# Block boundaries with rstd and the scaled product in PSUM, the residual add on VectorE, and sums of squares as float32 products

## The chip, the cores and the metric

One core of a Trainium2 chip runs the whole program. The metric is the time of one execution on the device, in microseconds (us). TensorE multiplies matrices from SBUF into PSUM (8 banks of 128 x 512 float32), VectorE and ScalarE work on SBUF and PSUM, GpSimd on SBUF; DMA queues bring the weights.

## What is computed

Two blocks follow each other on 512 tokens of width 1024, in float32. The first has two layers of this form, with four gains each:

```python
h = rms_norm(x, g[0])
m = parallel_conv_mla(h, ...) if i % 2 == 0 else conformer_conv(h, ...)
x = x + rms_norm(m, g[1])
h = rms_norm(x, g[2])
x = x + rms_norm(squared_relu_mlp(h, w1[i], w2[i]), g[3])
```

`rms_norm(x, g)` is `x * rsqrt(mean(x * x) + 1e-6) * g`, the mean over the 1024 channels. The second block is one layer with a forgetting attention, a pooled branch and a gated MLP; it takes the first block's `x`.

## The kernel before

Activations lie channel by channel: 8 tiles of 128 channels x 512 tokens. A product in float32 precision is three TensorE matmuls, because every operand is kept as a high part and a low part of a narrower format: high x high, high x low, low x high (`mm3`, L357 to L359). The split of an activation is a ScalarE copy that makes the high part (L397, or L400 with a scale) and a VectorE subtraction that makes the low part (L398, L401). Weights come by DMA as `raw`, and are split the same way (L284 on ScalarE, L286 on VectorE, in the conformer's stage on GpSimd) into nine buffers `W`.

`boundary` (L929) stands between two sublayers and runs four times: behind the attention (`mla`), behind the first MLP, behind the conformer, behind the second MLP. It gets the residual `x`, the sublayer's output `m` with its last three tiles still to be multiplied (`last`), and `acc`, the squares of the first five tiles, summed over the tiles. It works on the left 256 tokens (`LA`) and the right 256 (`LB`) in turn:

- TensorE multiplies the last three tiles for the left half, and starts on the first for the right half. The evacuations add their squares to `acc`; the third tile's squares stay apart (`sq[0]`).
- `parts` splits `acc` (L397, L398), `sums` (L960) multiplies the high part, the low part and `sq[0]` by a matrix of ones (L962, L963, L964): the sum over the channels stands in every partition.
- `rsqrts` (L405) makes `r = rsqrt(sum / 1024 + eps)`: ScalarE's table function (L450 through `fn`), then one Newton step in three VectorE instructions (L420, L422, L424).
- `update` (L967) forms `m * g * r` on VectorE (L970) and adds it to `x` (L973): on GpSimd for all left tiles, and for the right tiles 3, 5, 6, 7; on VectorE for the right tiles 0, 1, 2, 4 (`XB`). `update2` splits the new `x`, scaled by the next norm's gain, into `h` (L400, L401) and asks for one more block of weights.
- TensorE, done with the last three tiles, starts the next sublayer's first four weight tiles (`first`, in four PSUM banks): `kouter` runs over k = 0 to 7 for the left half, and behind k = 2 calls `hook`, then over k = 0 to 7 for the right half. `hook` holds the right half's sum, the left updates of tiles 4 to 7, the right rsqrt, the eight right updates, and the squares of the new `x`: `acc2`, left half added on GpSimd (L470), right half on VectorE.
- `acc2` gives the next sublayer its norm (`rs`) later, by `rstd_acc` and `colsum` (L459, L460), behind one more weight tile's 24 matmuls. Until then the first products wait unscaled in PSUM.

Instructions are put in each engine's order at compile time: among those whose inputs are ready by the compiler's own clock, the one written first goes first; each engine then runs its list strictly in order. A PSUM tile (`PS`) takes one of eight banks, and a bank is free when the tile's last reader is done. `S` are nine SBUF buffers of 128 x 544 for passing values.

Of the kernel before, what the change touches and what calls it, by code (L numbers as in the profile page):

```python
# [16 lines left out]
OP = mybir.AluOpType  # L17
# [4 lines left out]
T = 512  # L22
D = 1024
# [31 lines left out]
XA = ()  # L55
XB = (0, 1, 2, 4)
HK = 2
LA = slice(0, 256)
# [4 lines left out]
LB = slice(256, 512)  # L63
# [180 lines left out]

class Weights:
# [58 lines left out]
class Program:  # L304
# [100 lines left out]
    def rsqrts(self, jobs):  # L405
# [12 lines left out]
        stt = nc.vector.scalar_tensor_tensor  # L418
# [4 lines left out]
        for (s, n, out), q in zip(jobs, qs):  # L423
            stt(out=out, in0=q, scalar=1.5, in1=out, op0=OP.add, op1=OP.mult)  # L424

    def rsqrt(self, s, n, out):
        self.rsqrts([(s, n, out)])
        return out
# [500 lines left out]
    def boundary(self, x, m, acc, last, gi, nxt, first, extra=None):  # L929
# [8 lines left out]
        r, acc2 = self.S()[:, :T], self.S()[:, :T]  # L938
# [18 lines left out]
        def parts(cols):  # L957
            return self.split(self.P(), acc[:, cols], cols=256), sq[0]

        def sums(p, s):  # L960
            ps = self.PS()[:, :256]
            mm(ps, self.ones, p[:, 0, :256], start=True, stop=False)  # L962
            mm(ps, self.ones, p[:, 1, :256], start=False, stop=False)  # L963
            mm(ps, self.onesf, s, start=False, stop=True)  # L964
            return ps

        def update(k, cols):  # L967
            if cols is LA:
                h.append(self.P())
            V.scalar_tensor_tensor(out=m[k][:, cols], in0=m[k][:, cols], scalar=self.v("g", 8 * gi + k),  # L970
                                   in1=r[:, cols], op0=OP.mult, op1=OP.mult)
            eng = V if k in (XA if cols is LA else XB) else G
            ins = eng.tensor_add(out=x[k][:, cols], in0=x[k][:, cols], in1=m[k][:, cols]).ins  # L973
            if eng is G:
                self.last_update = ins
# [17 lines left out]
        s = sums(*parts(LA))  # L993
        tile(0, LB, slice(5, None), pb[0])
        self.rsqrt(s, D, r[:, LA])
# [5 lines left out]
        box = {"p": parts(LB)}  # L1001

        def hook():
            box["s"] = sums(*box["p"])
            updates(range(4, 8), LA)
            self.rsqrt(box["s"], D, r[:, LB])
            updates(range(8), LB)
            for k in range(8):
                self.square_into(acc2[:, LA], x[k][:, LA], k == 0, G)
            for k in range(8):  # L1010
                self.square_into(acc2[:, LB], x[k][:, LB], k == 0)
# [731 lines left out]
```

## Time and profile before

| | us |
|---|---|
| median of three runs (lowest, highest) | 1763.58 (1763.04, 1767.39) |
| the profiled execution | 1762.84 |
| its span, first to last instruction | 1761.1 |
| TensorE busy | 1724.0 (98%) |
| VectorE busy | 1091.2 (62%) |
| ScalarE busy | 801.6 (46%) |
| GpSimd busy | 274.0 (16%) |

Busy time of TensorE is modelled at the ends of its matmuls, so the starts are what to compare. A line number names the instruction's line in the kernel; a helper's line (L398, L401, L470) is shared by all its callers, and the tile names and shapes tell them apart. PE is TensorE, DVE VectorE, ACT ScalarE, POOL GpSimd. In a list in order of time, the bracket gives the engine's idle time before the instruction and what ended it. The four boundaries lie at about 218 to 264, 575 to 623, 785 to 830 and 1143 to 1192 us of the span.

### The profile page before, as it was taken

The numbers are of one execution on the slowest core, as the hardware profiler recorded it, in microseconds if no ns is written. First come the engines' busy times: TensorE is split into PE (matmuls) and PEld (weight loads), VectorE is DVE, ScalarE is ACT, GpSimd is POOL, SyncE is SP. The second block draws the span as 40 slices with busy tenths as digits, with TensorE's granted clock in tenths as the row PEclk, the third lists the DMA queues.
The fourth block names the chain that finished last, engine by engine and source line by source line (L and its number), as shares of the span: only waits on it lengthen the run. The fifth ranks groups of instructions, "written<-read, shape, count | busy, mean of one in ns | idle before, by whom it ended". The sixth has DMA issues, their size and how long they took to land.

```text
span 1761.1 us, 23142 instructions
## 1 busy us (share of the span) xinstructions
PE 1724.0 (98%) x8828; PEld 1460.4 (83%) x8828; DVE 1091.2 (62%) x1772; ACT 801.6 (46%) x1461; POOL 274.0 (16%) x339
## 2 busy tenths in 40 slices
PE   9999999999999999999999999989999999999999
PEld 7778898888888878999888888888787888888887
DVE  7988786344444789968544444488897655344452
ACT  6546655333333446676533333357665443232331
POOL 3513330000000365503000000051223200000000
PEclk9999999999999999999999999999999999999999
DMA  5231313222222133512322222222223222222221
GB/s 198 73 104 55 108 51 130 96 96 96 96 96 96 48 108 107 169 60 85 109 97 96 96 96 96 96 96 74 73 62 101 100 97 98 96 96 96 96 96 60
DMA packets 49887, 167.26 MB, mean 95 GB/s; under 512 B 6848, under 2 KB 7296, under 8 KB 49776
## 3 DMA queue, kind: packets, MB, share of 16 engines
q1 hardware_dynamic: 47776, 160.70, 27.9%
q0 software_dynamic: 1936, 5.07, 0.9%
q8 instruction: 69, 1.13, 0.3%
q14 instruction: 42, 0.34, 0.1%
q10 hardware_dynamic: 64, 0.02, 0.0%
HBM read 158.25 MB, written 4.19 MB: 92 GB/s over the span
## 4 chain that ended last, share of the span: by engine, by line
PE 81%; DVE 11%; issue 3%; ACT 2%; POOL 2%; DMA 1%; SPq 0%; POOLq 0%; ACTq 0%; DVEq 0%
PE ps L357 26%; PE ps L358 26%; PE ps L359 26%; DVE P L970 1%; PE ps L625 1%; DVE W L286 1%; POOL P L973 1%; DVE P L401 1%; DVE S L1479 1%; DVE S L424 1%; DVE P L398 1%; DVE S L422 1%; DMA raw<-in_w 1%; ACT S L450 0%; DVE S L420 0%
## 5 line engine op out<-in xcount | busy, mean ns | idle before, releaser
L357 PE MATMUL ps<-P,W 128*128 128x512 f32 (+1 forms) x2541 | 928.7, 366 | 4.9 <-DVE S L1132 2.8
L358 PE MATMUL ps<-P,W 128*128 128x512 f32 (+1 forms) x2541 | 925.7, 364 | 4.9 <-DVE P L401 4.9
L359 PE MATMUL ps<-P,W 128*128 128x512 f32 (+1 forms) x2541 | 923.9, 364 | 0.0
L284 ACT ACTIVATE W<-raw 128x512 fp32r<-128x512 f32 x578 | 356.6, 628 | 649.9 <-PE ps L359 608.5
L286 DVE TENSOR_TENSOR W<-raw,W 128x512 fp32r<-128x512 f32 x523 | 371.0, 717 | 378.7 <-ACT W L284 376.1
L357 PEld LDWEIGHTS ps<-P,W 128*128 128x128 f32 x2541 | 482.6, 190 | 82.5 <-DVE S L1132 3.2
L358 PEld LDWEIGHTS ps<-P,W 128*128 128x128 f32 x2541 | 482.7, 190 | 79.9 <-DVE P L401 5.7
L359 PEld LDWEIGHTS ps<-P,W 128*128 128x128 f32 x2541 | 482.6, 190 | 75.3 <-DVE W L286 0.2
L973 POOL TENSOR_TENSOR P<-P 128x256 f32<-128x256 f32 x48 | 46.7, 981 | 770.6 <-DVE P L970 769.5
L398 DVE TENSOR_TENSOR P<-S,P 128x512 fp32r<-128x512 f32 (+3 forms) x134 | 93.8, 706 | 50.4 <-ACT P L397 49.8
L397 ACT ACTIVATE P<-S 128x512 fp32r<-128x512 f32 (+3 forms) x134 | 81.5, 614 | 63.8 <-DVE S L1666 25.9
L286 POOL TENSOR_TENSOR W<-raw,W 128x512 fp32r<-128x512 f32 x55 | 72.9, 1348 | 38.1 <-ACT W L284 34.0
L1084 DVE SCALAR_TENSOR_TENSOR ps<-P,vec,ps 128x512 f32<-128x512 f32 x116 | 77.8, 744 | 0.0
L400 ACT ACTIVATE P<-P,vec 128x256 fp32r<-128x256 f32 (+1 forms) x80 | 43.7, 550 | 51.8 <-POOL P L973 31.4
L1031 DVE SCALAR_TENSOR_TENSOR S<-ps,S 128x512 f32<-128x512 f32 x64 | 43.6, 689 | 34.2 <-PE ps L359 34.1
L401 DVE SCALAR_TENSOR_TENSOR P<-P,vec 128x256 fp32r<-128x256 f32 (+1 forms) x80 | 54.3, 692 | 10.9 <-ACT P L400 10.7
L470 POOL TENSOR_TENSOR S<-S 128x256 f32<-128x256 f32 (+1 forms) x45 | 48.7, 1084 | 74.6 <-ACT S L469 72.2
L469 ACT ACTIVATE S<-P 128x256 f32<-128x256 f32 (+1 forms) x105 | 46.4, 472 | 17.4 <-DVE P L1058 11.4
L638 POOL TENSOR_TENSOR P<-S,P 128x512 fp32r<-128x512 f32 (+1 forms) x24 | 34.3, 1427 | 114.4 <-DVE P L637 108.5
L1051 DVE TENSOR_TENSOR P<-ps,P 128x512 f32<-128x512 f32 x42 | 29.0, 691 | 28.7 <-PE ps L359 28.7
L625 PE MATMUL ps<-P 128*128 128x512 f32 (+3 forms) x160 | 41.2, 376 | 2.2 <-DVE S L1445 0.9
L470 DVE TENSOR_TENSOR S<-S 128x256 f32<-128x256 f32 (+1 forms) x60 | 33.1, 551 | 14.4 <-ACT S L469 13.4
(264 smaller groups left out, 1299.8 us busy)
## 6 DMA issues: line engine op xcount, KB each, us to landing
raw<-in_w SPq DMA_DIRECT2D x286, 512.0 KB
P<-in_xT SPq DMA_DIRECT2D x8, 256.0 KB
P<-in_xT POOLq DMA_DIRECT2D x8, 256.0 KB, 5.3
keep<-P SPq DMA_DIRECT2D x8, 256.0 KB
P<-P SPq DMA_DIRECT2D x16, 128.0 KB
P<-keep POOLq DMA_DIRECT2D x8, 256.0 KB, 4.3
out<-P SPq DMA_DIRECT2D x7, 256.0 KB
raw<-in_w SPq DMA_DIRECT2D x2, 256.0 KB
```

What stands on the lines that cost most here:

```text
L284: nc.scalar.activation(out=w[:, 0, :cols], in_=r, func=AF.Copy)
L286: eng.tensor_sub(out=w[:, 1, :cols], in0=r, in1=w[:, 0, :cols].bitcast(F32))
L357: mm(ps, w[0], x[0], start=first, stop=False)
L358: mm(ps, w[0], x[1], start=False, stop=False)
L359: mm(ps, w[1], x[0], start=False, stop=last)
L397: nc.scalar.activation(out=hi, in_=src, func=AF.Copy)
L398: nc.vector.tensor_sub(out=lo, in0=src, in1=hi.bitcast(F32))
L401: nc.vector.scalar_tensor_tensor(out=lo, in0=src, scalar=scale, in1=hi.bitcast(F32), op0=OP.mult, op1=OP.subtract)
L470: (eng or nc.vector).tensor_add(out=acc, in0=acc, in1=t)
L625: mm(o[:m], k, q[:, pl, c0:], start=n == 0 and m == 128, stop=n == len(keys) - 1 and mask is None)
L973: ins = eng.tensor_add(out=x[k][:, cols], in0=x[k][:, cols], in1=m[k][:, cols]).ins
L1084: V.scalar_tensor_tensor(out=dst if dst is not None and t == taps[-1] else acc, in0=u, scalar=w, in1=acc, op0=OP.mult, op1=OP.add)
```

## The change

`r` becomes a PSUM tile; a second PSUM tile, `tm`, takes the product `m * g * r`, and `m` is no longer overwritten. The Newton steps work on an SBUF buffer and only the last writes `r`. The add to `x` is VectorE's for all tiles and both halves, reading `tm`. `sums` multiplies `acc` itself, unsplit, with the float32 ones, so that `parts` is gone; a float32 operand is not two matmuls here but one float32 product. The squares of the left half of the new `x` are added on VectorE too. In `boundary`, GpSimd has no instruction left.

```diff
--- before.py
+++ after.py
@@ -52,8 +52,6 @@
 WARM = 11
 TICK = (6, 3)
 AK = 7
-XA = ()
-XB = (0, 1, 2, 4)
 HK = 2
 LA = slice(0, 256)
 TABLES = [s.name for s in SETS]
@@ -242,6 +240,10 @@
 
 
 
+def size(cols):
+    return cols.stop - cols.start
+
+
 class Weights:
 
     AHEAD = 4
@@ -402,7 +404,7 @@
                                            op0=OP.mult, op1=OP.subtract)
         return p
 
-    def rsqrts(self, jobs):
+    def rsqrts(self, jobs, dst=None):
 
         nc = self.nc
         qs = [self.S()[:out.shape[0], :out.shape[1]] for _, _, out in jobs]
@@ -421,10 +423,10 @@
         for (s, n, out), q in zip(jobs, qs):
             stt(out=q, in0=q, scalar=-0.5 / n, in1=out, op0=OP.mult, op1=OP.mult)
         for (s, n, out), q in zip(jobs, qs):
-            stt(out=out, in0=q, scalar=1.5, in1=out, op0=OP.add, op1=OP.mult)
-
-    def rsqrt(self, s, n, out):
-        self.rsqrts([(s, n, out)])
+            stt(out=out if dst is None else dst, in0=q, scalar=1.5, in1=out, op0=OP.add, op1=OP.mult)
+
+    def rsqrt(self, s, n, out, dst=None):
+        self.rsqrts([(s, n, out)], dst)
         return out
 
 
@@ -935,7 +937,7 @@
         V, A, G, mm = nc.vector, nc.scalar, nc.gpsimd, nc.tensor.matmul
         self.norm_set = RSQRT
         self.tables(RSQRT)
-        r, acc2 = self.S()[:, :T], self.S()[:, :T]
+        r, tm, acc2 = self.PS(), self.PS(), self.S()[:, :T]
         h = []
         sq = {}
 
@@ -954,25 +956,20 @@
                 f(ps[:, cols], cols)
             return ps
 
-        def parts(cols):
-            return self.split(self.P(), acc[:, cols], cols=256), sq[0]
-
-        def sums(p, s):
-            ps = self.PS()[:, :256]
-            mm(ps, self.ones, p[:, 0, :256], start=True, stop=False)
-            mm(ps, self.ones, p[:, 1, :256], start=False, stop=False)
-            mm(ps, self.onesf, s, start=False, stop=True)
+        def sums(cols):
+            ps = self.PS()[:, :sq[0].shape[-1]]
+            mm(ps, self.onesf, acc[:, cols], start=True, stop=False)
+            mm(ps, self.onesf, sq[0], start=False, stop=True)
             return ps
 
         def update(k, cols):
             if cols is LA:
                 h.append(self.P())
-            V.scalar_tensor_tensor(out=m[k][:, cols], in0=m[k][:, cols], scalar=self.v("g", 8 * gi + k),
+
+            t = tm[:, cols]
+            V.scalar_tensor_tensor(out=t, in0=m[k][:, cols], scalar=self.v("g", 8 * gi + k),
                                    in1=r[:, cols], op0=OP.mult, op1=OP.mult)
-            eng = V if k in (XA if cols is LA else XB) else G
-            ins = eng.tensor_add(out=x[k][:, cols], in0=x[k][:, cols], in1=m[k][:, cols]).ins
-            if eng is G:
-                self.last_update = ins
+            V.tensor_add(out=x[k][:, cols], in0=t, in1=x[k][:, cols])
 
         def update2(k, cols):
             self.split(h[k], x[k][:, cols], self.v(nxt[0], nxt[1] + k), cols=cols)
@@ -990,23 +987,23 @@
             ps = tile(i, LA)
             evac(i, ps, LA)
         pb = [tile(0, LB, slice(0, 5))]
-        s = sums(*parts(LA))
+        s = sums(LA)
         tile(0, LB, slice(5, None), pb[0])
-        self.rsqrt(s, D, r[:, LA])
+        self.rsqrt(s, D, self.S()[:, :size(LA)], r[:, LA])
         updates(range(4), LA)
         for i in (1, 2):
             pb.append(tile(i, LB))
         for i in range(3):
             evac(i, pb[i], LB)
-        box = {"p": parts(LB)}
+        box = {}
 
         def hook():
-            box["s"] = sums(*box["p"])
+            box["s"] = sums(LB)
             updates(range(4, 8), LA)
-            self.rsqrt(box["s"], D, r[:, LB])
+            self.rsqrt(box["s"], D, self.S()[:, :size(LB)], r[:, LB])
             updates(range(8), LB)
             for k in range(8):
-                self.square_into(acc2[:, LA], x[k][:, LA], k == 0, G)
+                self.square_into(acc2[:, LA], x[k][:, LA], k == 0)
             for k in range(8):
                 self.square_into(acc2[:, LB], x[k][:, LB], k == 0)
 
```

## Rows read from the trace of the kernel before

**Rows 1.** TensorE's waits, whole span: line, releaser, us in total, times, longest.

```profile
PE ps L963 <- DVE P L398: 5.2, 4, 1.3
PE ps L358 <- DVE P L401: 4.9, 4, 2.2
PE ps L962 <- ACT P L397: 3.8, 4, 1.7
PE ps L357 <- DVE S L1132: 2.8, 1, 2.8
```

**Rows 2.** Busy table, hook of the first boundary: busy us by engine, granted clock, DMA.

```profile
240.00:245.00 5.00, 3.49 (x17) 2.92 (x16) 4.33 (x8) 1.98 (x5) 3.42 (x4) 0.77 0.14 57
```

**Rows 3.** TensorE's order of time, first boundary: start, us, line, tiles, [idle, releaser].

```profile
240.04 0.28 PE L358 MATMUL ps<-P,W 128*128 128x256 f32 x1
240.16 0.28 PE L359 MATMUL ps<-P,W 128*128 128x256 f32 x1
242.33 0.39 PE L963 MATMUL ps<-P,ones 128*128 128x256 f32 x1 [1.29 <-DVE P L398]
...
252.99 0.39 PE L358 MATMUL ps<-P,W 128*128 128x256 f32 x1 [1.02 <-DVE P L401]
```

**Rows 4.** TensorE's order of time, second and fourth boundary: both ends of the stretch.

```profile
597.17 0.28 PE L359 MATMUL ps<-P,W 128*128 128x256 f32 x1
...
611.12 0.39 PE L358 MATMUL ps<-P,W 128*128 128x256 f32 x1 [0.59 <-DVE P L401]
...
1163.21 0.28 PE L359 MATMUL ps<-P,W 128*128 128x256 f32 x1
...
1178.63 0.39 PE L358 MATMUL ps<-P,W 128*128 128x256 f32 x1 [2.20 <-DVE P L401]
```

**Rows 5.** TensorE's order of time, the first boundary's left sum.

```profile
228.58 0.28 PE L963 MATMUL ps<-P,ones 128*128 128x256 f32 x1
...
229.25 0.28 PE L358 MATMUL ps<-P,W 128*128 128x256 f32 x1
```

**Rows 6.** GpSimd's group of the residual adds, by line and form.

```profile
L973 POOL TENSOR_TENSOR P<-P 128x256 f32<-128x256 f32 x48 | 46.7, 981 | 770.6 <-DVE P L970 769.5 <-ACT S L469 1.1
```

**Rows 7.** VectorE's groups by line and form: count, busy us, mean ns, idle before.

```profile
L1084 DVE SCALAR_TENSOR_TENSOR ps<-P,vec,ps 128x512 f32<-128x512 f32 x116 | 77.8, 744 | 0.0
...
L970 DVE SCALAR_TENSOR_TENSOR P<-P,vec,S 128x256 f32<-128x256 f32 x64 | 41.0, 664 | 0.2
L401 DVE SCALAR_TENSOR_TENSOR P<-P,vec 128x256 fp32r<-128x256 f32 x64 | 38.7, 620 | 6.4 <-ACT P L400 6.3
L1051 DVE TENSOR_TENSOR P<-ps,P 128x512 f32<-128x512 f32 x42 | 29.0, 691 | 28.7 <-PE ps L359 28.7
L470 DVE TENSOR_TENSOR S<-S 128x256 f32<-128x256 f32 x44 | 22.1, 502 | 9.3 <-ACT S L469 8.5
...
L973 DVE TENSOR_TENSOR P<-P 128x256 f32<-128x256 f32 x16 | 10.7, 685 | 0.0
...
L1058 DVE TENSOR_TENSOR P<-ps,P 128x256 f32<-128x256 f32 x12 | 4.9, 421 | 6.0 <-PE ps L359 6.0
...
L422 DVE SCALAR_TENSOR_TENSOR S<-S 128x256 f32<-128x256 f32 x10 | 4.2, 424 | 0.3
...
L420 DVE SCALAR_TENSOR_TENSOR S<-ps,S 128x256 f32<-128x256 f32 x10 | 4.2, 417 | 5.4 <-ACT S L450 5.4
```

**Rows 8.** VectorE's order of time, first boundary, single instructions.

```profile
239.73 0.41 DVE L470 TENSOR_TENSOR S<-S 128x256 f32<-128x256 f32 x1
...
256.87 0.47 DVE L970 SCALAR_TENSOR_TENSOR P<-P,vec,S 128x256 f32<-128x256 f32 x1
```

**Rows 9.** ScalarE's order of time, first boundary, one head of `h`.

```profile
242.03 0.51 ACT L400 ACTIVATE P<-P,vec 128x256 fp32r<-128x256 f32 x1 [0.75 <-POOL P L973]
```

**Rows 10.** VectorE's and TensorE's order of time, sum behind the first boundary.

```profile
266.60 0.69 DVE L398 TENSOR_TENSOR P<-S,P 128x512 fp32r<-128x512 f32 x1
...
269.95 0.39 PE L459 MATMUL ps<-P,ones 128*128 128x512 f32 x1
```

## Prediction

> **What bounds the kernel now.** I read the views in this order. TensorE's own waits, longest first, show what a shorter chain could give back at all: three groups belong to `boundary` (the second product of the sum of squares waits for the split's low part, the second matmul of the right half waits for the low part of its first `h`, the first product of the sum waits for the split's high part), 5.2 + 4.9 + 3.8 = 13.9 us, each four times, once per boundary [rows 1]. Nothing else there is of the same size; the fourth line, 2.8 us, is the wait for `rs` in the stage behind the second boundary. Its other waits lie in stages that the change doesn't touch, so the boundaries are what to work out. [...] Matmuls of 256 columns follow each other by 0.12 us up to the hook (240.04, 240.16); then the sum's second product starts only at 242.33, and the low part of the first right-hand `h` lets TensorE go on at 252.99 [rows 3]. From the last matmul before the hook (240.16) to that start are 12.83 us. In the second boundary the same stretch is 13.95 us, in the fourth 15.42 [rows 4]; the third repeats the first (12.85).
>
> What has to be in that stretch: the matmul at its start 0.12, the sum, 5 x 4 x 3 = 60 matmuls of the left half at 0.12 = 7.20, and one matmul of the right half, 0.12.
>
> **The change, part by part.**
>
> *The sum of squares.* Removed: two products with `ones` (0.12 us each), and ahead of them a ScalarE copy and a VectorE subtraction. Added: one more float32 product. Its price is on record: at 228.58 the split's low product starts and at 229.25 the second matmul behind it, and between lie that product, the float32 product and one matmul; 0.67 - 0.24 = 0.43 us [rows 5]. The new sum is 0.86 us where the old was 0.67: 0.19 us dearer, eight times. The stretch after the change is then at least 0.12 + 0.86 + 7.20 + 0.12 = 8.30 us, and the four boundaries can give back 4.5 + 5.65 + 4.55 + 7.1 = 21.8 us, clock included. The other four sums (left half) already lie without a wait, and cost 4 x 0.19 = 0.8 us. Ceiling: 21.0 us.
>
> *The residual add moves from GpSimd to VectorE.* GpSimd's add takes 0.98 us in the mean [rows 6]; VectorE's with one PSUM operand takes 0.42 (L1058, an evacuation of the same shape) [rows 7]. For each update this shortens the chain product, add, ScalarE head, low part by 0.56 us and by one hand-over between engines. It also lengthens VectorE's queue: 48 adds and 28 additions of squares (7 in each boundary) come to it. But while GpSimd reads, VectorE is slowed: the product L970 takes 0.66 us in the mean and 0.47 when GpSimd rests (256.87); the add L973 0.69 against 0.42; the low part L401 0.62 against 0.47, the figure for the same form of instruction [rows 7, 8]. So VectorE's work: before, 41.0 + 38.7 + 22.1 + 10.7 = 112.5 us for L970, L401, L470 and L973 [rows 7]. After, 64 x (0.47 + 0.42 + 0.47) + 72 x 0.41 = 87.0 + 29.5 = 116.5 us, less eight subtractions of the split, 8 x 0.42 = 3.4: 113.1 us. The contention that goes pays for the work that comes. ScalarE issues the same heads and squares, less eight copies; no DMA is moved, and GpSimd's queue loses work only.
>
> *`r` and `tm` in PSUM.* The changed product doesn't occur in `boundary` before, but the convolution has its form at 512 columns, vector input and output in PSUM: 744 ns, 53 more than an add of 512 columns (691); the old product alone, all in SBUF, is 50 ns above an add of 256 columns (470 and 420) [rows 7, 8]. So the surcharge is the scalar's, not PSUM's, and I take nothing. Bounds: 53 ns each if it is PSUM's after all, on 12 instructions of each boundary's path 0.6 us; slightly below nothing from the rsqrt step that reads PSUM, 417 against 424 ns for the one that doesn't [rows 7]. [...]
>
> *The banks.* Two of eight PSUM banks are now held through the boundary. When the four `first` tiles open, `r`, `tm` and the second and third right-hand tile may still be held: exactly eight, if the first right-hand tile and the left sum have been read, which needs them only by the end of the 2 x 24 matmuls that follow. Cost taken: nothing; if that cover goes, the rival below prices it.
>
> *What is late next.* (a) At the hook TensorE needs the last addition of squares on the right half. In the first boundary it starts at 239.73, takes 0.41 [rows 8], and TensorE arrives at 240.28: no wait. Behind the two MLPs, where the evacuations too are VectorE's, L962 waited 1.7 of its 3.8 us each [rows 1]; the copy and its hand-over go, up to 0.8 of it can stay; I take 0.4, twice. (b) The first right-hand `h`. VectorE, free at 240.1, does four left updates (4 x 1.36 = 5.4), three rsqrt steps (3 x 0.42), product and add (0.89); ScalarE's head takes 0.51 [rows 9], the low part 0.47: 248.6 us, hand-overs left out. TensorE arrives at 240.16 + 8.30 = 248.5. So this wait is nearly gone, but not safely: I take 0.5 us, four times, bounds 0 and 1.5. Behind it VectorE needs 1.36 us for each k and TensorE 1.44: TensorE leads. (c) The sum for the next stage. Its low part started at 266.60 and TensorE asked for it at 269.95 at the earliest it could [rows 10]: 2.7 us of slack. TensorE now comes 4.5 us earlier, VectorE's squares about 3 to 4. I take 0.5 us for three boundaries; the one behind the second has its own stall, 2.8 us [rows 1], which I leave as it is (bounds: gone, or doubled).
>
> Sum: 21.0 - 0.8 - 2.0 - 1.5 = 16.7 us. The profiled execution took 1762.8 us, 1.7 above its span, and the median is 1763.6; from the median 16.7 us less is 1747.
>
> **Rivals.**
>
> *VectorE gets slightly behind, or the gain is given back later.* If the added squares or the weights' splits come between the updates in half the places, or the weight stream behind the boundary can't be had 4.5 us earlier, about half of the gain stays: 1755. For it: VectorE has no idle time in this stretch, and (b) is even to 0.1 us. Against it: buffers come free when TensorE frees them, so loads move with it.
>
> *The banks bind.* If the fourth `first` tile has to wait for the second right-hand tile, read behind the MLPs only just before the hook, TensorE stands there for up to 4 us in two boundaries: 16.7 - 8 leaves 1755 as well. Against it is the count above.
>
> *Slower: the right half becomes VectorE's.* If all 14 additions of squares and six weight splits (0.7 us each) are queued between the eight right-hand updates, a k takes 1.36 + (14 x 0.41 + 6 x 0.7)/8 = 2.6 us on VectorE where TensorE needs 1.44: 7 x 1.16 = 8 us more in each boundary, which with 16.7 given back is some 15 us slower, 1779. It decides from 2.0 us for each k on. For it: their adds no longer have an engine of their own. Against it: in the trace the updates come ahead of additions of squares that could have been done earlier.
>
> *The change doesn't do what it says*: the low part of `h` stays late by as much and only the sum's own waits go. Then 5.2 + 3.8 turn into a longer wait at the right half, and the time stays within 3 us: 1761.
>
> **How the numbers follow.** Forecast 0.68 (1741 to 1751); half given back by either of the first two rivals 0.19 (1751 to 1760, three quarters of it below 1758.3); no effect 0.06; slower 0.07. About 0.3%, 5.3 us, is what a measurement can tell from no change: faster is below 1758.3, slower above 1768.9. Faster 0.68 + 0.14 + 0.01 = 0.83, same 0.10, slower 0.07. The range reaches from the ceiling with a part of the 2.8 us stall (1741) to the half-way rival's middle (1757).
>
> **What would show it.** Right: in TensorE's waits L962 and L963 of before have no successor above 0.5 us, the low part's wait is below 1 us each, the granted clock stays 1.00 through the hook, the stretch is 8.3 to 9.5 us in each boundary, L970 and L401 stand at 0.47 us. Wrong: a product on PSUM above 0.5 us, waits of `first` tiles for evacuations, TensorE waiting for several k of the right half, or a new wait at L459 that takes the gain back.

## The result and the profile after

| | kernel before | changed kernel |
|---|---|---|
| median (range), us | 1763.67 (1763.04 to 1767.39) | 1745.64 (1742.04 to 1749.04) |
| profiled execution, us | 1762.84 | 1744.32 |
| its span, us | 1761.1 | 1742.6 |
| VectorE busy, us | 1091.2 | 1083.0 |
| GpSimd busy, us | 274.0 | 204.7 |

The ratio is 0.990 (95% interval 0.9877 to 0.9923), 18.0 us less. A second measurement beside other kernels gave 0.9901 [0.9884, 0.9919], again with a median of 1745.64 us.

Where a line of the code has moved, its new number is: the three matmuls L359 to L361, the two products of the sum L961 and L962, product L970, addition L972, head and low part of `h` L402 and L403, addition of squares L472, rsqrt steps L422, L424, L426, the next norm's sum L461 and L462, weight split L286 (ScalarE) and L288 (VectorE or GpSimd).

TensorE's waits over the whole span of the changed kernel (line, releaser, us in total, times, longest), which answer to [rows 1]:

```profile
PE ps L461 <- ACT P L399: 4.5, 3, 1.9
PE ps L360 <- DVE P L403: 3.8, 4, 1.6
PE ps L359 <- DVE P L639: 2.7, 1, 2.7
```

The waits of the sum's two first products are gone, and so is the 2.8 us wait for `rs` behind the second boundary. Of the first line, 3.3 us lie in the first 100 us, which the change doesn't touch (1.3 us in the kernel before, 2.9 in the second trace of the changed kernel); the other 1.2 lie behind the fourth boundary and are new. The second line is what is left of the right half's waits: 3.5 of its 3.8 us lie in the second boundary, the rest at the start of the program. The third lies in another stage and stands in the kernel before as well. Below the lines shown, one wait in the conformer's stage (of L1192 for ScalarE) has grown from 1.4 to 2.3 us.

The busy table of the first boundary's hook in the changed kernel (busy us of PE, PEld, DVE, ACT and POOL, granted clock, DMA share, GB/s), which answers to [rows 2]:

```profile
240.00:245.00 5.00, 5.00 (x41) 4.89 (x40) 4.78 (x13) 2.27 (x6) 0.00 (x0) 1.00 0.19 75
```

TensorE is busy for the whole 5 us, where it was 3.49, and the granted clock, a share of full speed, is 1.00, where it had been 0.77 (0.50 from 243 to 246 us, behind the idle time).

TensorE's order of time there in the changed kernel (start, us, line, tiles), which answers to [rows 3]:

```profile
242.03 0.28 PE L361 MATMUL ps<-P,W 128*128 128x256 f32 x1
242.15 0.60 PE L961 MATMUL ps<-S,onesf 128*128 128x256 f32 x2
242.59 0.59 PE L962 MATMUL ps<-S,onesf 128*128 128x256 f32 x2
242.83 0.47 PE L359 MATMUL ps<-P,W 128*128 128x256 f32 x1
243.14 0.28 PE L360 MATMUL ps<-P,W 128*128 128x256 f32 x1
...
250.21 0.28 PE L359 MATMUL ps<-P,W 128*128 128x256 f32 x1
250.33 0.28 PE L360 MATMUL ps<-P,W 128*128 128x256 f32 x1
```

No row of this stretch has idle time before it. From the last matmul before the hook to the second of the right half are 250.33 - 242.03 = 8.30 us, the least that the prediction allowed; it had been 12.83. The same two matmuls lie 8.30 us apart in each of the other three boundaries.

VectorE's groups in the changed kernel (count, busy us, mean ns of one, idle before), which answer to [rows 7]:

```profile
L403 DVE SCALAR_TENSOR_TENSOR P<-P,vec 128x256 fp32r<-128x256 f32 x64 | 33.9, 529 | 0.3
L472 DVE TENSOR_TENSOR S<-S 128x256 f32<-128x256 f32 x72 | 32.8, 455 | 8.9 <-ACT S L471 8.5
L970 DVE SCALAR_TENSOR_TENSOR ps<-P,vec,ps 128x256 f32<-128x256 f32 x64 | 31.0, 485 | 0.4
L972 DVE TENSOR_TENSOR P<-ps,P 128x256 f32<-128x256 f32 x64 | 26.8, 419 | 0.1
```

Product and addition, which have one of their operands in PSUM (`ps`), stand at 0.485 and 0.419 us. The low part and the addition of squares, which read SBUF alone, are dearer in the mean than their 0.47 and 0.41 us, and the second boundary is where: 0.67 and 0.56 us in the mean there, 0.48 and 0.42 in the other three.

**Where the time went, boundary by boundary.** The same matmul is looked up in both traces, and the difference of its start is what has been gained up to there.

| matmul | before, us | after, us | gained so far | in this step |
|---|---|---|---|---|
| first of 256 columns, first boundary | 218.02 | 219.70 | -1.68 | -1.68 |
| the same, second boundary | 575.04 | 572.39 | 2.65 | 4.33 |
| behind the second boundary, just ahead of the 2.83 us stall | 633.46 | 630.14 | 3.32 | 0.67 |
| behind that stall, granted clock 1.00 again | 642.98 | 634.90 | 8.08 | 4.76 |
| left sum, third boundary | 794.24 | 787.04 | 7.20 | -0.88 |
| first of 256 columns, fourth boundary | 1141.08 | 1129.55 | 11.53 | 4.33 |
| fourth boundary, ahead of the sum behind it | 1192.18 | 1173.92 | 18.26 | 6.73 |
| first of the forgetting attention (L625, then L627) | 1241.7 | 1225.4 | 16.3 | -2.0 |
| end of the span | 1761.1 | 1742.6 | 18.5 | 2.2 |

The four boundaries themselves give back 4.33 + 0.67 + 4.33 + 6.73 = 16.1 us. The end of the stall behind the second is worth 4.76: the 2.83 us of waiting, and 1.9 of the slower matmuls behind it (granted clock 0.78 in 637 to 640 us of the kernel before and 0.66 in 640 to 643). The longer wait in the conformer's stage takes 0.9 back, the sum behind the fourth boundary and what follows it 2.0. From the first row to the forgetting attention this comes to 17.9 us, and to 18.0 in the second trace of the changed kernel. What lies ahead of the first boundary is no effect of the change: that matmul starts between 217.7 and 221.3 us in the traces of before, of the changed kernel and of the experiments, and at 221.20 in the second trace of the changed kernel itself. Of the 2.2 us in the last block, 1.1 fall where the kernel before waits 0.84 us for a DMA (at 1297.77), and 1.2 at 1344 to 1353, where both kernels have the same waits and the granted clock is lower for longer in the kernel before (0.60 from 1344.51 to 1353.05, 0.77 over the same matmuls in the changed kernel, 1327.22 to 1334.58). In the traces of the experiments the last block gives 1.9 to 4.5 us on this trace of the kernel before, and 2.9 with the adds still on GpSimd: no run ties it to the change.

**The stall behind the second boundary.** The prediction left its 2.8 us as they were. TensorE's and ScalarE's order of time in the kernel before:

```profile
628.48 0.39 PE L460 MATMUL ps<-P,ones 128*128 128x512 f32 x1
637.13 0.50 PE L357 MATMUL ps<-P,W 128*128 128x512 f32 x1 [2.83 <-DVE S L1132]
...
632.89 0.63 ACT L284 ACTIVATE W<-raw 128x512 fp32r<-128x512 f32 x1 [3.85 <-DMA raw<-in_w]
633.43 0.67 ACT L450 ACTIVATE S<-ps,eps 128x512 f32<-128x512 f32 x1
```

The sum is done at 628.9, but its rsqrt (L450) stands on ScalarE behind a weight copy (L284), and that one waits 3.85 us for its block's DMA. In the changed kernel ScalarE waits for no block there:

```profile
625.58 0.69 ACT L452 ACTIVATE S<-ps,eps 128x512 f32<-128x512 f32 x1 [1.81 <-PE ps L462]
```

The step is 4.75 us in every run below whose residual adds are VectorE's, and 3.3 where they stay on GpSimd. Moving the residual adds is thus enough to end the stall, which makes it one more effect of GpSimd's additions. The plain sums alone leave 1.18 us of it. Which of the queues in between makes the block late, no run separates.

**The second boundary** is the one that falls short. TensorE's order of time there, in the changed kernel; its three waits for the low part of `h`:

```profile
607.41 0.39 PE L360 MATMUL ps<-P,W 128*128 128x256 f32 x1 [1.34 <-DVE P L403]
...
615.40 0.39 PE L360 MATMUL ps<-P,W 128*128 128x256 f32 x1 [0.53 <-DVE P L403]
...
618.73 0.39 PE L360 MATMUL ps<-P,W 128*128 128x256 f32 x1 [1.63 <-DVE P L403]
```

GpSimd's and VectorE's order of time over the same microseconds:

```profile
604.35 1.29 POOL L288 TENSOR_TENSOR W<-raw,W 128x512 fp32r<-128x512 f32 x1 [396.32 <-DVE P L403]
605.81 1.26 POOL L288 TENSOR_TENSOR W<-raw,W 128x512 fp32r<-128x512 f32 x1 [0.16 <-ACT W L286]
608.65 1.30 POOL L288 TENSOR_TENSOR W<-raw,W 128x512 fp32r<-128x512 f32 x1 [1.59 <-ACT W L286]
...
604.57 1.36 DVE L472 TENSOR_TENSOR S<-S 128x256 f32<-128x256 f32 x1
605.85 0.48 DVE L970 SCALAR_TENSOR_TENSOR ps<-P,vec,ps 128x256 f32<-128x256 f32 x1
606.25 1.10 DVE L403 SCALAR_TENSOR_TENSOR P<-P,vec 128x256 fp32r<-128x256 f32 x1
...
608.67 0.41 DVE L972 TENSOR_TENSOR P<-ps,P 128x256 f32<-128x256 f32 x1
```

Beside a weight split on GpSimd, VectorE's two instructions that read two SBUF operands take 1.10 and 1.36 us; the two that read one of their operands from PSUM keep 0.48 and 0.41. In the kernel before, the first of these weight splits started at 616.44, since GpSimd's residual adds stood ahead of it; now it starts at 604.35, in the middle of the right half. GpSimd's order of time in the kernel before:

```profile
615.56 0.92 POOL L973 TENSOR_TENSOR P<-P 128x256 f32<-128x256 f32 x1 [0.76 <-DVE P L970]
616.44 1.48 POOL L286 TENSOR_TENSOR W<-raw,W 128x512 fp32r<-128x512 f32 x1
```

### The profile page after: what moved, and what is told of

It reads as the page before. It is cut to its first block, busy times and chain, and to the rows that moved or that the text cites. A ratio compares the mean times of both kernels' runs of the same rounds, so it can differ in the third digit from the quotient of the medians.

```text
span 1742.6 us, 23105 instructions
## 1 busy us (share of the span) xinstructions
PE 1712.4 (98%) x8828; PEld 1450.2 (83%) x8828; DVE 1083.0 (62%) x1840; ACT 800.7 (46%) x1453; POOL 204.7 (12%) x263
## 4 chain that ended last, share of the span: by engine, by line
PE 76%; DVE 18%; ACT 3%; issue 2%; DMA 1%; SPq 0%; POOL 0%; ACTq 0%; DVEq 0%
PE ps L359 25%; PE ps L361 24%; PE ps L360 24%; DVE ps L1081 4%; DVE W L288 2%; PE ps L627 1%; DVE P L403 1%; DVE P L400 1%; DMA raw<-in_w 1%; DVE S L1476 1%; DVE S L472 1%; DVE ps L970 1%; DVE P L972 1%; ACT S L452 1%; DVE S L424 1%
## 5 line engine op out<-in xcount | busy, mean ns | idle before, releaser
L359 PE MATMUL ps<-P,W 128*128 128x512 f32 (+1 forms) x2541 | 917.7, 364 | 3.0 <-ACT P L402 1.2
L361 PE MATMUL ps<-P,W 128*128 128x512 f32 (+1 forms) x2541 | 918.1, 362 | 0.0
L286 ACT ACTIVATE W<-raw 128x512 fp32r<-128x512 f32 x578 | 359.1, 630 | 652.8 <-PE ps L361 609.5
L288 DVE TENSOR_TENSOR W<-raw,W 128x512 fp32r<-128x512 f32 x523 | 367.7, 709 | 380.9 <-ACT W L286 377.9
L360 PEld LDWEIGHTS ps<-P,W 128*128 128x128 f32 x2541 | 478.7, 188 | 80.0 <-DVE P L403 5.7
L359 PEld LDWEIGHTS ps<-P,W 128*128 128x128 f32 x2541 | 476.0, 188 | 79.2 <-ACT P L402 1.6
L361 PEld LDWEIGHTS ps<-P,W 128*128 128x128 f32 x2541 | 478.6, 188 | 75.2 <-DVE W L288 0.4
L288 POOL TENSOR_TENSOR W<-raw,W 128x512 fp32r<-128x512 f32 x55 | 73.2, 1352 | 439.4 <-DVE P L403 396.3
L400 DVE TENSOR_TENSOR P<-S,P 128x512 fp32r<-128x512 f32 (+2 forms) x126 | 88.9, 711 | 47.8 <-ACT P L399 47.3
L399 ACT ACTIVATE P<-S 128x512 fp32r<-128x512 f32 (+2 forms) x126 | 78.3, 627 | 53.1 <-DVE S L1663 25.9
L402 ACT ACTIVATE P<-P,vec 128x256 fp32r<-128x256 f32 (+1 forms) x80 | 44.0, 550 | 35.4 <-DVE P L972 27.3
L471 ACT ACTIVATE S<-P 128x256 f32<-128x256 f32 (+1 forms) x105 | 47.9, 475 | 18.5 <-DVE P L1055 12.5
L472 DVE TENSOR_TENSOR S<-S 128x256 f32<-128x256 f32 (+1 forms) x88 | 43.8, 497 | 14.0 <-ACT S L471 13.4
L403 DVE SCALAR_TENSOR_TENSOR P<-P,vec 128x256 fp32r<-128x256 f32 (+1 forms) x80 | 49.4, 619 | 4.7 <-ACT P L402 4.3
L627 PE MATMUL ps<-P 128*128 128x512 f32 (+3 forms) x160 | 41.2, 375 | 1.4 <-DVE S L1442 0.9
L452 ACT ACTIVATE S<-ps 128x512 f32<-128x512 f32 (+2 forms) x56 | 31.8, 580 | 19.9 <-PE ps L630 9.6
L1030 ACT ACTIVATE S<-S 128x512 f32<-128x512 f32 x64 | 39.2, 618 | 0.3 <-DVE S L1028 0.2
```

The source lines that it names most:

```text
L286: nc.scalar.activation(out=w[:, 0, :cols], in_=r, func=AF.Copy)
L288: eng.tensor_sub(out=w[:, 1, :cols], in0=r, in1=w[:, 0, :cols].bitcast(F32))
L359: mm(ps, w[0], x[0], start=first, stop=False)
L360: mm(ps, w[0], x[1], start=False, stop=False)
L361: mm(ps, w[1], x[0], start=False, stop=last)
L399: nc.scalar.activation(out=hi, in_=src, func=AF.Copy)
```

## The experiments

Each ratio is to the kernel before, measured on the same chip beside it, with its 95% interval. Line numbers are those of the changed kernel, except in the first experiment.

**The plain sums alone** (kernel before, with the changed sums).

```diff
-            mm(ps, self.ones, p[:, 0, :256], start=True, stop=False)
-            mm(ps, self.ones, p[:, 1, :256], start=False, stop=False)
-            mm(ps, self.onesf, s, start=False, stop=True)
+            mm(ps, self.onesf, acc[:, cols], start=True, stop=False)
+            mm(ps, self.onesf, sq[0], start=False, stop=True)
...
```

> The kernel before with the plain float32 sum alone; the residual adds and the squares stay on GpSimd, r in SBUF. Theory (two causes, the sum's split at the hook and the update chain through GpSimd at the right half): the waits on the split, 9.0 us together, go, but the right half's first low part comes only some 1 us earlier than before while TensorE is there 2 to 3 us earlier, so its wait grows from 4.9 us in all to 10 or more; the time falls by 3 to 6 us, to about 1759. Rival (the split is the whole cause, and with it the lower clock): the right half's wait does not grow, the time falls by 12 us or more, to 1751 or below.

Measured: 1758.51 us, 0.9988 [0.9978, 0.9997], some 2 us below the kernel before beside it and short of the 3 to 6 expected. TensorE's waits:

```profile
PE ps L358 <- DVE P L401: 8.0, 7, 2.1
PE ps L357 <- ACT P L400: 3.6, 5, 1.6
```

The waits at the sum went, but for 2.5 us behind the two MLPs, and those at the first right-hand `h` grew from 4.9 to 10.3 us (the other 1.3 us of the two lines lie elsewhere). The stretch takes 11.6 to 13.5 us, where it took 12.8 to 15.4: the chain through GpSimd's additions still sets its end. That is the shape of the prediction's last rival, and its size.

**The adds without the plain sums** (changed kernel, sums split as before).

```diff
+        def parts(cols):
+            return self.split(self.P(), acc[:, cols], cols=256), sq[0]
+
-        def sums(cols):
+        def sums(p, s):
...
-            mm(ps, self.onesf, acc[:, cols], start=True, stop=False)
-            mm(ps, self.onesf, sq[0], start=False, stop=True)
+            mm(ps, self.ones, p[:, 0, :256], start=True, stop=False)
+            mm(ps, self.ones, p[:, 1, :256], start=False, stop=False)
+            mm(ps, self.onesf, s, start=False, stop=True)
...
```

> The changed kernel with the sum of before: acc is split, and its high and low part are multiplied. Everything else as changed. Theory: the two waits of the sum come back, 1.5 us in the first and third boundary and 1.5 to 3 in the others, with the lower clock behind them for some microseconds (about 1 us each); the right half's first low part is late by the same and waits little. The time is 7 to 11 us above the changed kernel, about 1754. Rival (the sum costs nothing once GpSimd is out of the way, because VectorE gets to the split's low part at once): within 3 us of the changed kernel. Rival (the split is the whole cause): within 5 us of the kernel before.

Measured: 1745.73 us, 0.9912 [0.9897, 0.9927]. The theory fell. TensorE's order of time at the first boundary's hook:

```profile
240.75 0.28 PE L361 MATMUL ps<-P,W 128*128 128x256 f32 x1
240.87 0.28 PE L964 MATMUL ps<-P,ones 128*128 128x256 f32 x1
240.99 0.28 PE L965 MATMUL ps<-P,ones 128*128 128x256 f32 x1
241.11 0.60 PE L966 MATMUL ps<-S,onesf 128*128 128x256 f32 x2
```

The split sum follows without a wait. Its subtraction takes 0.42 us in the mean here. In the kernel before it took 0.94 beside GpSimd's adds, and started behind two products that were slowed as well (VectorE's order of time in that kernel):

```profile
240.07 1.35 DVE L970 SCALAR_TENSOR_TENSOR P<-P,vec,S 128x256 f32<-128x256 f32 x2
241.34 0.94 DVE L398 TENSOR_TENSOR P<-S,P 128x256 fp32r<-128x256 f32 x1
```

So the 9.0 us of waits at the sum, which the prediction put down to the split, were GpSimd's too. The split isn't quite free: behind the fourth boundary the wait for the sum is 2.1 us, where it is 1.2 in the changed kernel.

**SBUF in place of PSUM** (changed kernel).

```diff
-        r, tm, acc2 = self.PS(), self.PS(), self.S()[:, :T]
+        r, acc2 = self.S()[:, :T], self.S()[:, :T]
...
-            t = tm[:, cols]
+            t = m[k][:, cols]
```

> The changed kernel with r in SBUF and the product m*g*r written over m in SBUF, as before; the add is VectorE's as changed. Theory: where GpSimd is idle (first, third and fourth boundary) nothing changes: no wait in the stretch from the hook to the right half, the product at 0.48 us and the add at 0.42. In the second boundary, where GpSimd splits weights during the right half, product and add are slowed too, and TensorE's 3.5 us of waits there grow to 5 to 9 us. In all 1 to 5 us above the changed kernel. Rival (the place in PSUM is what makes the updates fast): product or add above 0.5 us in every boundary, and 6 us or more above the changed kernel. Rival (PSUM is dear, and SBUF would be faster): below the changed kernel.

Measured: 1741.22 us, 0.9884 [0.9869, 0.9899], not above the changed kernel (0.9901 [0.9884, 0.9919]). Its product takes 0.524 us in the mean, its addition 0.415, the low part 0.475; no boundary but the second has a wait in its right half, 0.56 and 0.47 us. The theory (1 to 5 us above) fell. GpSimd's weight splits slow the products here (0.67 us in the mean in the second boundary) and not the low parts, and TensorE waits less for it. By itself the place of `r` and of the product doesn't carry the gain.

**The left half's squares back on GpSimd** (changed kernel).

```diff
-                self.square_into(acc2[:, LA], x[k][:, LA], k == 0)
+                self.square_into(acc2[:, LA], x[k][:, LA], k == 0, G)
```

> The changed kernel with the left half's squares of the new x added on GpSimd, as before. Theory: each boundary again has about 6 us of GpSimd reading SBUF, in which VectorE's low parts and additions with two SBUF inputs take twice as long, but product and add, with one operand in PSUM, do not; VectorE is spared seven additions. The right half's first low part is 0.5 to 1.5 us late in each boundary: 0 to 5 us above the changed kernel. Rival (GpSimd's presence alone slows everything on VectorE, PSUM or not): product and add above 0.6 us while it runs, and 8 us or more above.

Measured: 1745.88 us, 0.9912 [0.9897, 0.9927]. GpSimd's and VectorE's order of time in the first boundary:

```profile
245.31 6.13 POOL L472 TENSOR_TENSOR S<-S 128x256 f32<-128x256 f32 x7 [37.38 <-ACT S L471]
...
246.36 0.86 DVE L426 SCALAR_TENSOR_TENSOR ps<-S 128x256 f32<-128x256 f32 x1
247.13 0.96 DVE L403 SCALAR_TENSOR_TENSOR P<-P,vec 128x256 fp32r<-128x256 f32 x1
248.02 0.48 DVE L970 SCALAR_TENSOR_TENSOR ps<-P,vec,ps 128x256 f32<-128x256 f32 x1
248.53 0.42 DVE L972 TENSOR_TENSOR P<-ps,P 128x256 f32<-128x256 f32 x1
```

While GpSimd adds its seven squares, the last rsqrt step and the low part, which read SBUF alone, take twice their time; product and addition keep theirs. TensorE's waits for the low part come to 5.1 us in nine, none above 0.8. What GpSimd does in this stretch costs little in the median; the runs further down show that it would cost more without the operand in PSUM.

**The weight splits of the second boundary off GpSimd** (changed kernel; the first eight that GpSimd would make behind this boundary go to VectorE).

```diff
-        self.on_pool = range(self.loc["pw1", 7, 9][0] + 1, self.loc["pw2", 0, 0][0])
+        self.on_pool = range(self.loc["pw1", 7, 9][0] + 9, self.loc["pw2", 0, 0][0])
```

> The changed kernel, with the first eight weight blocks that GpSimd splits (those that fall into the right half of the second boundary) split by VectorE instead. Theory (TensorE's three waits of 3.5 us in the second boundary's right half are VectorE's low parts and squares slowed by GpSimd's reads): the low parts there go back to 0.48 us, the waits fall below 1 us, and the boundary is like the first and the third; 1 to 4 us below the changed kernel. Rival (VectorE is simply full there): eight splits of 0.6 us more make the waits longer, and the time is 1 to 4 us above.

Measured: 1737.67 us, 0.9863 [0.9848, 0.9878]. The busy table over the second boundary's right half, and VectorE's groups of the two forms that read SBUF alone:

```profile
600.00:620.00 20.00, 20.00 (x141) 18.07 (x140) 19.50 (x46) 11.98 (x26) 1.41 (x1) 1.00 0.28 85
```

```profile
L403 DVE SCALAR_TENSOR_TENSOR P<-P,vec 128x256 fp32r<-128x256 f32 x64 | 30.6, 478 | 0.6 <-ACT P L402 0.2
L472 DVE TENSOR_TENSOR S<-S 128x256 f32<-128x256 f32 x72 | 30.0, 417 | 8.7 <-ACT S L471 8.5
```

In the changed kernel the same 20 us read:

```profile
600.00:620.00 20.00, 16.33 (x124) 14.95 (x123) 19.82 (x39) 11.24 (x26) 9.45 (x8) 1.00 0.26 86
```

TensorE stands still for 3.67 us of these in the changed kernel and for none here, though VectorE got eight splits more; low part and squares fall to the price of the other boundaries. GpSimd's weight splits, not VectorE's amount of work, made the second boundary's waits. The gain of 8 us is more than the 1 to 4 expected: by the traces the second boundary gives 5.1 us where it gave 0.7, and the conformer's wait is back at 1.4 us; all between the first boundary and the last block comes to 4.9 us, and the other 3.1 lie where the traces scatter, ahead of the first boundary and in the last block.

**One more addition on VectorE for each right-hand update** (changed kernel; the result goes to a part of `tm` that nobody reads any more).

```diff
+            if cols is LB:
+                V.tensor_add(out=tm[:, LA], in0=r[:, LA], in1=x[k][:, LB])
             self.split(h[k], x[k][:, cols], self.v(nxt[0], nxt[1] + k), cols=cols)
```

> The changed kernel with one more addition of 256 columns on VectorE (0.33 us) in each of the eight right-half updates of each boundary, into a part of tm that nobody reads; the result is unaffected. It asks how near VectorE is to setting the boundary. In the changed kernel one k of the right half takes VectorE 1.45 us and TensorE 1.44. Theory (even, no slack): most of the 32 x 0.33 = 10.6 us shows, 5 to 11 us above the changed kernel, as waits of the second matmul in the right half or of the sum behind it. Rival (slack from the matmuls of the next weight tile that were drawn into the right half): 0 to 4 us.

Measured: 1745.40 us, 0.9912 [0.9897, 0.9927]. The median shows no cost for the 32 additions, 8 x 0.33 = 2.6 us by their pitch in each boundary. The trace does: the first and the third boundary give back 3.1 us each, where they gave 4.3, and the fourth 3.8 where it gave 6.7, 1.5 of which return behind it. That is 3.8 us in all, within the rival's 0 to 4, and in the profiled execution 1.6 us ahead of the first boundary and 1.7 in the last block make up for it. More than half of the additions' time is covered; VectorE's slack is smaller than one addition for each k.

**Three more** (the same addition three times).

```diff
+            if cols is LB:
+                for _ in range(3):
+                    V.tensor_add(out=tm[:, LA], in0=r[:, LA], in1=x[k][:, LB])
```

> As the kernel with one more addition, with three (1.0 us for each k). Theory (the slower rival of the forecast, a right half that is VectorE's): a k takes 2.45 us on VectorE where TensorE needs 1.44; 7 x 1.0 = 7 us in each boundary, 28 to 34 us above the changed kernel, which makes it 10 us or more slower than the kernel before. Rival (part of it is hidden by matmuls drawn forward): 12 to 22 us above the changed kernel.

Measured: 1781.18 us, 1.0107 [1.0094, 1.0121]. TensorE's waits:

```profile
PE ps L359 <- ACT P L402: 27.7, 25, 1.7
```

Here the right half is VectorE's: 25 waits for the 32 heads of `h`. The 35 us over the changed kernel are the slower rival's mechanism; the changed kernel itself stands at its edge.

**The changed kernel once more**, beside the next two.

> The changed kernel once more, without an edit, beside the next two on one chip. Theory (the gain is the boundaries' and doesn't hang on the chip): a ratio of 0.988 to 0.992 to the kernel before, some 1744 to 1746 us. Rival (the first look flattered or harmed it): outside of that.

Measured: 1745.64 us, 0.9901 [0.9884, 0.9919]. In its trace the second boundary's three waits stand again, 1.33, 0.53 and 1.64 us, where they had been 1.34, 0.53 and 1.63.

**SBUF and the moved weight splits together** (both diffs above).

> Both edits that came out below the changed kernel at once: r and the scaled product in SBUF, and the eight weight splits of GpSimd behind the second boundary's start on VectorE. Theory: GpSimd's reads of SBUF in the second boundary are the one thing left that costs time there, and without them the place of r and of the product makes no difference: the time is that of the run with the splits alone moved, 1736 to 1740 us. Rival (the two gains are separate and add, 4.5 and 8 us): 1731 to 1735 us. Rival (SBUF operands cost by themselves, and the PSUM placement pays once the splits are gone): 1741 us or more.

Measured: 1739.58 us, 0.986 [0.984, 0.988], on the same chip as the run before this one (1745.64). Once GpSimd is out of the second boundary the place of `r` and of the product makes no difference that can be measured (0.9863 with PSUM); no boundary has a wait in its right half. This and the run with the splits alone moved are the fastest kernels of the study.

**The adds alone** (kernel before; the residual add on VectorE, and nothing else of the change but an SBUF buffer of its own for the Newton steps; `t` is `m[k][:, cols]`, so the product still overwrites `m`).

```diff
...
-            eng = V if k in (XA if cols is LA else XB) else G
-            ins = eng.tensor_add(out=x[k][:, cols], in0=x[k][:, cols], in1=m[k][:, cols]).ins
-            if eng is G:
-                self.last_update = ins
+            V.tensor_add(out=x[k][:, cols], in0=t, in1=x[k][:, cols])
...
```

> The kernel before with nothing but the residual add moved from GpSimd to VectorE: the sums stay split, r and the product stay in SBUF, the squares of the left half stay on GpSimd. Theory (the add's move carries the whole gain; PSUM, the plain sums and the squares' engine are each worth 2 us or less): 1741 to 1748 us. Rival (the parts stand in for each other, so that each can be undone alone but not all three together): 1750 to 1757 us, with TensorE waiting at the sum for the split's low part as before.

Measured: 1751.98 us, 0.9935 [0.992, 0.9951]. Neither of the two was right: the time is the rival's, and the sum has no wait above 0.3 us. The waits stand at the right half instead, and VectorE's and GpSimd's order of time in the first boundary shows why:

```profile
245.14 6.42 POOL L472 TENSOR_TENSOR S<-S 128x256 f32<-128x256 f32 x7 [37.26 <-ACT S L471]
...
246.49 0.96 DVE L426 SCALAR_TENSOR_TENSOR S<-S 128x256 f32<-128x256 f32 x1
247.49 1.73 DVE L974 SCALAR_TENSOR_TENSOR P<-P,vec,S 128x256 f32<-128x256 f32 x2
249.14 1.82 DVE L976 TENSOR_TENSOR P<-P 128x256 f32<-128x256 f32 x2
```

GpSimd now adds the left half's squares just when the first right-hand `h` is made. The products (L974 here, two in 1.73 us) and additions (L976, two in 1.82), all their operands in SBUF, take 0.85 to 0.96 us each. Where they have an operand in PSUM they don't, as the run with the squares on GpSimd shows. Two more runs put this to the test.

**SBUF, and the left squares on GpSimd** (changed kernel, with the two diffs above; the sums stay plain).

> The changed kernel with r and the product in SBUF and the left half's squares on GpSimd; the sums stay plain products. Theory (with the product and the addition reading SBUF alone, VectorE is slowed while GpSimd adds squares at the start of the right half, and PSUM is what shields the run that has only the squares on GpSimd): 1749 to 1753 us, L970 and L972 near 0.9 us each beside the additions on GpSimd, TensorE waiting 1 to 2 us for the first right-hand h in the first and third boundary. Rival (it is the split sum that made the kernel with the adds alone slow): 1741 to 1746 us and no such wait.

Measured: 1750.78 us, 0.9941 [0.9924, 0.9957]. TensorE's order of time, first boundary:

```profile
252.70 0.39 PE L360 MATMUL ps<-P,W 128*128 128x256 f32 x1 [1.68 <-DVE P L403]
```

**The split sums, and the left squares on GpSimd** (changed kernel; `r` and the product stay in PSUM).

> The changed kernel with the sums split as before and the left half's squares on GpSimd; r and the product stay in PSUM. Theory (PSUM shields VectorE, and the split costs little): 1745 to 1748 us, L970 and L972 at 0.48 and 0.42 us beside GpSimd. Rival (the split sum is what slows the kernel with the adds alone, by its copy and its subtraction on VectorE): 1749 to 1753 us.

Measured: 1747.69 us, 0.9919 [0.9904, 0.9934]. L970 and L972 (L974 and L976 here) take 0.482 and 0.415 us in the mean; the wait for the first right-hand `h` in the first boundary is 0.70 us, with one of 0.64 behind it, where it is 1.68 in SBUF. So with squares on GpSimd it is PSUM that pays (1745.9 and 1747.7 against 1750.8 and 1752.0), and the sum's form hardly does (1745.9 against 1747.7, 1750.8 against 1752.0, each pair within its intervals). The intervals of the medians with and without PSUM touch as well; the traces tell them apart. What each trace gives back between the first boundary and the forgetting attention, by the matmuls of the table of starts, in us:

| kernel | gain on the kernel before |
|---|---|
| changed kernel, two traces | 17.9, 18.0 |
| plain sums alone | 1.8 |
| adds without the plain sums | 15.4 |
| SBUF in place of PSUM | 18.1 |
| left squares on GpSimd, PSUM | 16.0 |
| left squares on GpSimd, PSUM, split sums | 15.1 |
| left squares on GpSimd, SBUF | 10.4 |
| adds alone (left squares on GpSimd, SBUF, split sums) | 10.1 |
| one more addition; three more | 14.1; -19.3 |
| weight splits moved; with SBUF | 22.8; 24.9 |

The adds by themselves are worth 10 of the 18 us. Most of the rest needs either PSUM or the left squares off GpSimd: with the squares on VectorE the place makes no difference (17.9 and 18.1), and with them on GpSimd it makes 5 to 6.

## Why the prediction came out

The forecast was 1747.0, the time is 1745.64. The mechanism is the one it named, the chain through GpSimd's additions and what they did to VectorE. That the sum came so close is partly luck, for its terms were less exact:

| step | forecast, us | measured, us |
|---|---|---|
| first boundary | 4.5 - 0.2 - 0.5 - 0.5 = 3.3 | 4.33 |
| second, its stall, conformer's stage | 5.65 - 0.2 - 0.4 - 0.5 = 4.55 | 0.67 + 4.76 - 0.88 = 4.55 |
| third | 4.55 - 0.2 - 0.5 - 0.5 = 3.35 | 4.33 |
| fourth | 7.1 - 0.2 - 0.4 - 0.5 - 0.5 = 5.5 | 6.7 - 2.0 = 4.8 |
| start of the program | 0 | -1.7 |
| last block | 0 | 2.2 |
| sum | 16.7 | 18.5 |

Without the end of the stall, for which nothing had been forecast, the time would have been about 1750.4, at the end of the forecast's range.

- *The sum of squares.* Right in price: from the sum's start to the second matmul behind it are 243.14 - 242.15 = 0.99 us, less one matmul 0.87, where 0.86 was worked out. Wrong in its part: the waits at the sum were taken for the split's. With the split in place and GpSimd out, they are gone as well (1745.73), and with the split gone and GpSimd in place the waits only move (1758.51).
- *The hook, (a).* Forecast 0.4 us twice, measured none: the sum starts 0.12 us behind the last matmul in all four boundaries. The addition of squares that it needs was late behind the MLPs because of GpSimd's residual adds: with nothing but those moved, the sum doesn't wait either.
- *The first right-hand `h`, (b).* Forecast 0.5 us four times, measured none. The mis-sized term is VectorE's time for one update: durations were added, 0.47 + 0.42 + 0.47 = 1.36 us, but an instruction starts before the one ahead of it has ended. VectorE's order of time in the changed kernel's first boundary:

```profile
248.55 0.48 DVE L970 SCALAR_TENSOR_TENSOR ps<-P,vec,ps 128x256 f32<-128x256 f32 x1
248.94 0.48 DVE L403 SCALAR_TENSOR_TENSOR P<-P,vec 128x256 fp32r<-128x256 f32 x1
249.34 0.42 DVE L972 TENSOR_TENSOR P<-ps,P 128x256 f32<-128x256 f32 x1
249.67 0.42 DVE L472 TENSOR_TENSOR S<-S 128x256 f32<-128x256 f32 x1
250.00 0.49 DVE L970 SCALAR_TENSOR_TENSOR ps<-P,vec,ps 128x256 f32<-128x256 f32 x1
```

  The starts lie 0.39, 0.40, 0.33 and 0.33 us apart. An update takes 1.12 us, and with the addition of squares that stands in each of them 1.45, against TensorE's 1.44. The low part of the first right-hand `h` (248.94) is done at 249.42, 0.9 us ahead of TensorE's 250.33. The kernel before showed this as well: in [rows 8] the addition starts at 239.73 and takes 0.41, and the next instruction on VectorE starts at 240.07.
- *Contention that goes pays for the work that comes.* True of the total, but mis-sized: the four groups take 33.9 + 32.8 + 31.0 + 26.8 = 124.5 us where 116.5 was worked out. All instructions had been given their price beside a resting GpSimd. It doesn't rest in the second boundary, which makes some 5.4 of the 8 us (16 low parts at 0.67 instead of 0.48, 18 additions at 0.56 instead of 0.42): GpSimd's queue, of which the prediction said only that it loses work, now reaches its weight splits 12 us sooner. With eight of them moved, low part and squares fall from 33.9 + 32.8 to 30.6 + 30.0 us and that boundary gives 4.45 us more. Here "what is late next" had an answer that was not on the list. That the second row of the table meets its forecast to the hundredth is luck, two errors that cancel: the boundary gave 0.67, with 3.5 us of new waits, and the end of the stall, which had been left as it was, 4.76.
- *PSUM operands.* Nothing was taken for them, and nothing it is: L970 0.485 us and L972 0.419 with PSUM, against the 0.47 and 0.42 of the forecast, and 0.482 and 0.422 in SBUF with the weight splits moved.
- *The banks.* No `first` tile waits for a bank. That rival, and the one of half the gain, are out.
- *The sum behind, (c).* Forecast 0.5 us in three boundaries, measured no wait in the first three and 1.23 + 0.22 us behind the fourth, where 2.0 us are lost in all. With `r` and the product in SBUF the first of these waits is 0.25 us (0.27 with the splits moved); no run shows why it is longer with PSUM.
- *Slower.* Its place was right and its threshold is real: one more addition for each k costs 3.8 us by the traces, three cost 35 us. The changed kernel was not far from it.

Left open: which queue made the weight block late that held up the sum behind the second boundary (with the plain sums alone the stall is 1.18 us and the block's wait 4.6), and the 2.2 us of the last block.

## What to carry over

Ask of an engine that shares work with a busy one not how long its instructions take, but what it does to the other: the residual add was slow itself, and it made the sums, the products and the low parts around it late. When work leaves such a queue, look at what moves up in it, and beside whom it will run then. An operand in PSUM is a shield against that: 5 to 6 us by the traces with GpSimd adding squares as the first right-hand `h` is made (4 to 5 by the medians), and no gain with those squares on VectorE. And where a median can't tell two kernels apart, the same matmul looked up in both traces can: here the two traces of the changed kernel agree within 0.1 us from the first boundary to the last block, while their starts differ by 1.5.

## What the runs showed of the hardware

VectorE's instructions of 256 columns follow each other by 0.33 us (addition) and 0.39 to 0.40 us (with a scalar), though each lasts 0.41 and 0.48: a sum of durations overstates a full queue by a fifth.

An instruction of VectorE with two SBUF operands, 0.41 to 0.48 us by itself, takes up to 1.05 us beside GpSimd's additions of 256 columns and up to 1.52 beside its weight splits of 512 (a low part, at 617.15 in the changed kernel); one with a PSUM operand stays at 0.48 (product) or 0.41 (addition), at most 0.49 and 0.43 over the 64 of each in the changed kernel. The second boundary of the changed kernel shows it (1.10 and 1.36 us against 0.48 and 0.41 beside GpSimd's weight splits), and so does the first boundary with the left squares on GpSimd (0.86 and 0.96 against 0.48 and 0.42).
